# Output stage of a two-layer hybrid decoder: loads six items ahead, a written order on two engines, and weight sums spread over more ticks

## The chip, the cores and the metric

The kernel runs on one core of one Trainium2 chip. Its time is that of one execution on the device in microseconds; less is better. Five engines work side by side: TensorE (PE) multiplies matrices into PSUM, VectorE (DVE) and ScalarE (ACT) do elementwise work, GpSimd (POOL) does more of it, and SyncE (SP) issues the transfers (DMA). Each engine takes its instructions in the order in which they stand in its own queue, and waits at an instruction until what it needs is there.

## The reference

For each of two layers, with D_MODEL = SEQ = 1024 and D_INNER = 2048:

```python
h = rmsnorm(x, norm_g[l]) * (1.0 + scale[:, None, :]) + shift[:, None, :]
p = h @ w_in[l]
...                       # y_m: four mLSTM heads of 256, y_r: four retention heads of 256
y = jnp.concatenate([y_m, y_r], axis=-1) @ w_out[l]
x = x + gate[:, None, :] * y
```

At the end stands `rmsnorm(x, final_g)`. What the change touches is above all the product with `w_out[l]` (2048 x 1024), the sum into `x`, and the preparation of `w_out`.

## The kernel before, in words

*Precision.* Every factor is split into a high and a low half: ScalarE casts the high half (line 599), another engine subtracts it from the value (line 600). `mm3` then issues three matmuls, high x high, high x low and low x high (lines 134, 135, 136), 128 x 128 against 128 x 512.

*Heads.* A layer works through eight head groups: 0 to 3 are mLSTM, 4 to 7 retention. Each projects its columns of `w_in`, whose tiles come in through the tag `raw` (four buffers) and are split into `wH` and `wL` (six buffers each), and puts its y rows into DRAM (`ydr`). Loops advance a clock by ticks. Work that isn't urgent is a generator which `launch` puts in a list; it says at each `yield n` that it wants to go on n ticks later. A group of the later ones is some 32 ticks long.

*Weight sums.* The output product is computed by a scheme of seven products of half-size blocks in place of eight. It needs sums of blocks of `w_out`; `weight_sums` (line 899) forms these during the heads from tiles of the tag `g` (six buffers), which gates and y rows use too. Each of its 8 rounds has 5 steps with `yield 2`, so 80 ticks; it starts after group 3. Sums for products 5 and 6 go to `tdr`; for products 3, 7 and 4 both halves go to `tsp`.

*Output stage.* `out_projection` runs the products in the order 1, 2, 5, 6, 3, 7, 4. Each has eight items (one y tile and one weight tile each), and an item is 12 matmuls, three into each of four PSUM banks. Products 1 and 2 use the banks b1, products 5, 6 and 3 the banks b2, products 7 and 4 the banks b3. At a product's end its banks are copied (`save`, `sum_up`) or go into x rows (`out_rows`): multiply by the gate, add to the old x, store, square for the next norm. In `out_units` the last two items go bank by bank, so that a bank is finished, emptied and used by the next product while others are still at work.

`OutPrep` prepares the items. `stage` does all for one item at once: the load or sum of its y tile, the split of it, the loads of the weights and, where no halves are stored, their split. Three items are prepared before the first is taken, and `take` prepares one and hands out one. The weights of products 1, 2, 5 and 6 use `raw` (line 983) and split into `wH`/`wL`; stored halves are loaded into `wH`/`wL` straight away (line 979). y tiles come into the pool `b` of 62 tiles (line 943).

*Order.* TensorE's order is written out. The order of the other engines, SP's among them, is set by a planner that simulates the program on a timeline and puts each instruction at its estimated time; which buffers a tag has and which instruction waits for which release follow from it. `tc.manual_schedule(engines=...)` puts the named engines' instructions in the order of the program's text instead.

Of the kernel before, what the change touches and what calls it, by code (L numbers as in the profile page):

```python
# [69 lines left out]
def tile_hybrid_trunk(ctx, tc, x, c, positions, w_ada, b_ada, norm_g, w_in, conv_w, conv_b,  # L70
# [62 lines left out]
    def mm3(o, lt, rt, start, stop, more=False):  # L133
# [28 lines left out]
    tdr = [[[dpool.tile([P, HALF], F32, name=f"tdr{l}_{j}_{k}") for k in range(KT)] for j in range(8)]  # L162
           for l in range(DEPTH)]
    SPLIT = (3, 7, 4)
    tsp = [{p: [[dpool.tile([P, HALF], F32, name=f"tsp{l}_{p}_{k}_{w}") for w in range(2)] for k in range(KT)]
            for p in SPLIT} for l in range(DEPTH)]
    sdr = [[dpool.tile([P, HALF], F32, name=f"sdr{l}_{k}") for k in range(14)] for l in range(DEPTH)]
# [430 lines left out]
    def split_to(dst, src, eng=G):  # L598
        A.copy(dst[0], src)  # L599
        eng.tensor_tensor(dst[1], src, f(dst[0]), ALU.subtract)  # L600
# [295 lines left out]
                Q.dma_start(sdr[l][k], other)  # L896
            yield 2

    def weight_sums(l):
# [12 lines left out]
        for i in range(KT):  # L912
            w11, w12 = load(i, 0), load(i, 1)
            yield 2
            w22 = load(8 + i, 1)
            V.tensor_tensor(w11, w12, w11, ALU.subtract)
            Q.dma_start(tdr[l][5][i], w11)
            yield 2
            V.tensor_tensor(w12, w22, w12, ALU.subtract)
            V.tensor_tensor(w11, w22, w11, ALU.subtract)  # L920
            Q.dma_start(tdr[l][6][i], w11)
            keep(w22, 3, i)
            yield 2
            keep(w12, 7, i)
            w21 = load(8 + i, 0)
            yield 2
            V.tensor_tensor(w21, w21, w11, ALU.subtract)
            keep(w21, 4, i)
            yield 2

    class OutPrep:
        ORDER = (1, 2, 5, 6, 3, 7, 4)

        def __init__(self, l):
            self.l, self.ready = l, []
# [13 lines left out]
        def split(self, src, tiles):  # L949
            split_to(tiles, src, V)  # L950
            return tiles

        def stage(self, n=1):
            l, sub = self.l, ALU.subtract
            for p, i in self.todo[:n]:
                if p == 1:
                    src = self.y(i, 0)
                elif p == 2:
                    self.y12[i] = src = self.y(8 + i, 0)
                elif p == 5 and i < 6:  # L960
                    src = self.load(sdr[l][8 + i])
                elif p == 5:
                    src = self.load(ydr[l][i][1])
                    self.y22[i] = self.y(8 + i, 1)
                    V.tensor_tensor(src, src, self.y22[i], ALU.add)
                elif p == 6:
                    self.s2[i] = src = bt()
                    V.tensor_tensor(src, self.y22[i], self.s3[i], sub)
                elif p == 3:
                    src = self.y12[i]  # L970
                    V.tensor_tensor(src, src, self.s2[i], sub)
                else:
                    src = self.s3[i] if p == 7 else self.y22[i]
                y2 = self.split(src, (bt(F32R), bt(F32R)))
                last = p == 4 and i >= KT - 2
                w2 = (bt(F32R), bt(F32R)) if last else (wt("wH", 512, 6, F32R), wt("wL", 512, 6, F32R))
                if p in SPLIT:
                    for which in range(2):
                        Q.dma_start(f(w2[which]), tsp[l][p][i][which])
                else:  # L980
                    raw = wt("raw", 512, 4)
                    rows = slice((i if p == 1 else 8 + i) * P, (i + 1 if p == 1 else 9 + i) * P)
                    Q.dma_start(raw, w_out[l, rows, 0:512] if p < 3 else tdr[l][p][i])
                    self.split(raw, w2)
                self.ready.append((y2, w2))
                if self.early and (p > 1 or i > 3):
                    res, k, src = self.early.pop(0)
                    res[k] = self.load(src)
            del self.todo[:n]

        def take(self):
# [38 lines left out]
    def out_rows(l, half, cc, tt, bank, gb, xnew, ss, xr, copy=False):  # L1030
        row = half * 4 + tt
        tmp = wt("th", 512, 5)
        if copy:
            A.copy(tmp, bank)
        add_gated(xr, tmp if copy else bank, gb[cc], tmp)
# [15 lines left out]
    def out_projection(l, prep, gb, fg, nhT):  # L1051
# [10 lines left out]
        x12, x22, x21 = [None] * 4, [None] * 4, [None] * 4  # L1062
        b1 = [ps_p() for _ in range(4)]
        run_units(out_units(prep, b1, True, False, save(b1, c1, None)))
        x11 = [residual(l, 0, 0, tt) for tt in range(4)]
        run_units(out_units(prep, b1, False, True,
                            lambda tt: out_rows(l, 0, 0, tt, b1[tt], gb, xn[0], ss[0], x11[tt])))
# [3 lines left out]
        def sum_up(tt):  # L1071
# [128 lines left out]
    for l in range(DEPTH):  # L1200
# [85 lines left out]
        for hg in range(8):  # L1286
# [23 lines left out]
            if hg == 7:  # L1310
                run_units(gate_path(l, hg, hT, gp, 0, 1))
                loads = OutPrep(l)
                loads.stage(2)
                run_units(gate_path(l, hg, hT, gp, 1))
                loads.stage(1)
# [46 lines left out]
```

## Time and profile before

| | us |
|---|---|
| three runs, median | 2334.56 (2332.99 to 2337.56) |
| profiled execution, its own time | 2333.26 |
| its span in the trace | 2331.6 |
| TensorE busy | 2268.6 (97%) |
| VectorE busy | 1459.2 (63%) |
| ScalarE busy | 959.7 (41%) |
| GpSimd busy | 815.0 (35%) |

In the span, layer 0's output stage lies from about 1016 to 1191 us, layer 1's from about 2125 to the last matmul at 2321 us; the heads lie ahead of each. In rows of instructions, `L1059` is the line, `pp<-wH,b` what is written and read, `x2` how many were put together, and the brackets at the end give the idle time ahead of it and what ended that.

### The profile page before, as it was taken

The numbers are of one execution on the slowest core, as the hardware profiler recorded it, in microseconds if no ns is written. First come the engines' busy times: TensorE is split into PE (matmuls) and PEld (weight loads), VectorE is DVE, ScalarE is ACT, GpSimd is POOL, SyncE is SP. The second block draws the span as 40 slices with busy tenths as digits, with TensorE's granted clock in tenths as the row PEclk, the third lists the DMA queues.
The fourth block names the chain that finished last, engine by engine and source line by source line (L and its number), as shares of the span: only waits on it lengthen the run. The fifth ranks groups of instructions, "written<-read, shape, count | busy, mean of one in ns | idle before, by whom it ended". The sixth has DMA issues, their size and how long they took to land.

```text
span 2331.6 us, 35126 instructions
## 1 busy us (share of the span) xinstructions
PE 2268.6 (97%) x12405; PEld 1946.5 (83%) x12405; DVE 1459.2 (63%) x2971; ACT 959.7 (41%) x1868; POOL 815.0 (35%) x777
## 2 busy tenths in 40 slices
PE   5999999999999999999999999999999999999998
PEld 4878888889878989887878888888898888889876
DVE  7386678566685655557755765564656665555685
ACT  5535434444432333345344544444444333324452
POOL 0344344334353444310063434334433443442000
PEclk9999999999999999999999999999999999999999
DMA  7234434454675763566733334333447666535765
GB/s 246 70 79 118 120 91 144 112 180 129 210 247 188 248 194 99 168 197 197 251 108 77 75 106 123 104 113 104 135 136 243 198 210 216 151 104 179 244 208 180
DMA packets 385729, 367.52 MB, mean 158 GB/s; under 512 B 82421, under 2 KB 268541, under 8 KB 385553
## 3 DMA queue, kind: packets, MB, share of 16 engines
q1 hardware_dynamic: 385552, 365.28, 52.0%
q8 instruction: 97, 1.59, 0.3%
q14 instruction: 80, 0.65, 0.1%
HBM read 253.99 MB, written 111.18 MB: 157 GB/s over the span
## 4 chain that ended last, share of the span: by engine, by line
PE 66%; DVE 9%; DMA 9%; issue 6%; POOL 4%; ACT 3%; SPq 2%; POOLq 0%; DVEq 0%; ACTq 0%
PE pp L134 17%; PE pp L135 17%; PE pp L136 17%; PE pa L134 4%; PE pa L136 4%; PE pa L135 4%; DMA g<-in_w_out_dram 2%; POOL b L600 1%; DVE acc L617 1%; POOL wL L600 1%; DMA g<-gdr 1%; PE pa L751 1%; DMA b<-ydr 1%; DMA ndr<-zt 1%; DMA b<-in_w_ada_dram 1%
## 5 line engine op out<-in xcount | busy, mean ns | idle before, releaser
L134 PE MATMUL pp<-b,wH 128*128 128x512 f32 x1792 | 713.5, 398 | 1.1 <-ACT b L1232 1.1
L135 PE MATMUL pp<-b,wH 128*128 128x512 f32 x1792 | 709.1, 396 | 0.6 <-DVE b L1235 0.6
L136 PE MATMUL pp<-b,wL 128*128 128x512 f32 x1792 | 709.5, 396 | 0.0
L600 POOL TENSOR_TENSOR wL<-raw,wH 128x512 fp32r<-128x512 f32 x274 | 374.0, 1373 | 405.5 <-ACT wH L599 338.6
L136 PEld LDWEIGHTS pp<-b,wL 128*128 128x128 f32 x1792 | 338.7, 189 | 80.7
L134 PEld LDWEIGHTS pp<-b,wH 128*128 128x128 f32 x1792 | 339.2, 189 | 73.3 <-issue 1.5
L135 PEld LDWEIGHTS pp<-b,wH 128*128 128x128 f32 x1792 | 339.1, 189 | 72.9 <-DVE b L1235 1.4
L134 PE MATMUL pp<-wH,b 128*128 128x256 f32 (+1 forms) x1136 | 348.5, 307 | 5.6 <-ACT acc L1059 4.3
L136 PE MATMUL pp<-wH,b 128*128 128x256 f32 (+1 forms) x1136 | 347.3, 306 | 0.0
L135 PE MATMUL pp<-wL,b 128*128 128x256 f32 (+1 forms) x1136 | 346.5, 305 | 0.0
L600 POOL TENSOR_TENSOR b<-acc,b 128x256 fp32r<-128x256 f32 (+1 forms) x208 | 212.6, 1039 | 281.4 <-ACT b L599 277.6
L599 ACT CAST wH<-raw 128x512 fp32r<-128x512 f32 x338 | 207.5, 617 | 177.6 <-PE pp L135 113.1
L134 PEld LDWEIGHTS pp<-wH,b 128*128 128x128 f32 x1136 | 214.6, 189 | 17.6 <-ACT acc L1059 5.6
L136 PEld LDWEIGHTS pp<-wH,b 128*128 128x128 f32 x1136 | 214.2, 189 | 10.8
L135 PEld LDWEIGHTS pp<-wL,b 128*128 128x128 f32 x1136 | 214.4, 189 | 10.4
L617 DVE SCALAR_TENSOR_TENSOR acc<-pp,cols,acc 128x511 f32<-128x511 f32 (+2 forms) x192 | 142.3, 741 | 25.0 <-ACT acc L612 22.8
L599 ACT CAST b<-acc 128x256 fp32r<-128x256 f32 (+1 forms) x208 | 94.5, 486 | 131.3 <-DVE acc L694 82.3
L600 POOL TENSOR_TENSOR sL<-th,sH 128x384 fp32r<-128x384 f32 x64 | 67.9, 1061 | 127.2 <-ACT sH L599 118.8
L600 DVE TENSOR_TENSOR b<-b,b 128x512 fp32r<-128x512 f32 x112 | 78.2, 714 | 47.5 <-ACT b L599 47.1
L1104 POOL TENSOR_TENSOR rs<-s,mhalf 128x4 f32<-128x4 f32 (+1 forms) x9 | 7.8, 872 | 270.9 <-DVE s L1103 270.9
L134 PE MATMUL pa<-b,b 128*128 128x256 f32 (+1 forms) x320 | 91.7, 286 | 7.8 <-ACT nd L797 7.4
L600 POOL TENSOR_TENSOR cL<-cf,cH 128x516 fp32r<-128x516 f32 (+1 forms) x48 | 64.8, 1350 | 90.5 <-ACT cH L599 90.5
(287 smaller groups left out, 3796.8 us busy)
## 6 DMA issues: line engine op xcount, KB each, us to landing
raw<-in_w_in_dram SPq DMA_DIRECT2D x274, 256.0 KB
b<-in_w_ada_dram SPq DMA_DIRECT2D x96, 256.0 KB
tsp<-g SPq DMA_DIRECT2D x96, 256.0 KB
gdr<-g SPq DMA_DIRECT2D x64, 256.0 KB
ndr<-zt SPq DMA_DIRECT2D x128, 128.0 KB
g<-ndr SPq DMA_DIRECT2D x64, 256.0 KB
g<-gdr SPq DMA_DIRECT2D x64, 256.0 KB
g<-in_w_out_dram SPq DMA_DIRECT2D x64, 256.0 KB
```

The source lines that it names most:

```text
L134: PE.matmul(o, lt[0], rt[0], start=start, stop=False, skip_group_check=more)
L135: PE.matmul(o, lt[0], rt[1], start=False, stop=False, skip_group_check=more)
L136: PE.matmul(o, lt[1], rt[0], start=False, stop=stop, skip_group_check=more)
L599: A.copy(dst[0], src)
L600: eng.tensor_tensor(dst[1], src, f(dst[0]), ALU.subtract)
L617: V.scalar_tensor_tensor(acc[:, d:], pt[:, 0:HALF - d], wcol, acc[:, d:], ALU.mult, ALU.add)
L751: PE.matmul(pd, kk[i][:, jo + P:jo + CH], qd, start=dt == 0 and i == 0, stop=dt == 1 and i == 1)
L1104: G.tensor_tensor(rs[:, 0:n], s, mhalf[:, 0:n], ALU.pow)
```

## The change

1. `OutPrep.stage` becomes four steps, `fetch`, `sum_up`, `cast` and `low`, each with a queue behind it (`got`, `summed`, `halved`, `ready`). `fetch` issues the loads of up to three more items than before. Weights and stored halves are loaded into the pool `b`, no longer into `raw`, `wH` or `wL`; only the splits of products 1, 2, 5 and 6 use `wH`/`wL`.
2. After product 1 the steps move one item on (`sum_up` twice, `cast` once), so that from then on the sum, the cast and the low half of one item belong to different calls of `take`.
3. From there to the first row of product 4's end, VectorE and ScalarE follow the order of the text.
4. Product 7's banks are all copied by ScalarE at once; the rows they go into are worked through later, one per tick (`corner_later`).
5. `weight_sums` takes its pace as an argument: 3 ticks a step from after group 3 in layer 0 (120 ticks), 5 ticks a step from after group 1 in layer 1 (200 ticks).

The number of instructions of each engine and the bytes moved are the same in both.

```diff
-            yield 2
+            yield pace
...
-                    raw = wt("raw", 512, 4)
                     rows = slice((i if p == 1 else 8 + i) * P, (i + 1 if p == 1 else 9 + i) * P)
-                    Q.dma_start(raw, w_out[l, rows, 0:512] if p < 3 else tdr[l][p][i])
-                    self.split(raw, w2)
-                self.ready.append((y2, w2))
+                    w2 = self.load(w_out[l, rows, 0:512] if p < 3 else tdr[l][p][i])
+                self.got.append((p, i, src, w2))
...
+        def cast(self):
+            if not self.summed:
+                return
+            p, src, w2 = self.summed.pop(0)
+            halves = [(src, (bt(F32R), bt(F32R)))]
+            if p not in SPLIT:
+                halves.append((w2, (wt("wH", 512, 6, F32R), wt("wL", 512, 6, F32R))))
+                w2 = halves[1][1]
+            for x, t in halves:
+                A.copy(t[0], x)
+            self.halved.append((halves, (halves[0][1], w2)))
+
+        def low(self):
+            if not self.halved:
+                return
+            halves, ready = self.halved.pop(0)
+            for x, t in halves:
+                V.tensor_tensor(t[1], x, f(t[0]), ALU.subtract)
+            self.ready.append(ready)
...
         def take(self):
-            self.stage()
+            self.fetch(2 if len(self.got) < AHEAD else 1)
+            for step in (self.sum_up, self.cast, self.low):
+                step()
             return self.ready.pop(0)
...
         run_units(out_units(prep, b1, True, False, save(b1, c1, None)))
+        for step in (prep.sum_up, prep.sum_up, prep.cast):
+            step()
+        ordered = tc.manual_schedule(engines={mybir.EngineType.DVE, mybir.EngineType.Activation})
+        ordered.__enter__()
...
-        run_units(out_units(prep, b3, True, False,
-                            lambda tt: out_rows(l, 1, 1, tt, b3[tt], gb, xn[1], ss[1], x22[tt], True)))
+        corner = [None] * 4
+
+        def read_out(tt):
+            corner[tt] = wt("th", 512, 5)
+            A.copy(corner[tt], b3[tt])
+
+        def corner_later():
+            for tt in range(4):
+                out_rows(l, 1, 1, tt, corner[tt], gb, xn[1], ss[1], x22[tt], corner[tt])
+                yield 1
+
+        run_units(out_units(prep, b3, True, False, read_out))
+        launch(corner_later())
 
         def end(tt):
+            if tt == 0:
+                ordered.__exit__(None, None, None)
...
-            if hg == 3:
-                launch(weight_sums(l))
+            if hg == (1 if l else 3):
+                launch(weight_sums(l, 5 if l else 3))
```

How this moves instructions is seen at three places. Lines from the diff on are renumbered: 943 is 944 after, 979 is 966, 685 to 695 are 686 to 696, 916 to 920 are 917 to 921.

SP's queue in product 1 of layer 0, before (`ydr` are y tiles, `sdr` sums of them, `in_w_out_dram` output weights):

```order
L943 DMA b_2191_11695<-ydr0_10_0_245 128x512
L983 DMA raw_2233_11852<-in_w_out_dram 128x512
L943 DMA b_2197_11707<-sdr0_6_511 128x512
L943 DMA b_2214_11787<-ydr0_11_0_247 128x512
L983 DMA raw_2242_11883<-in_w_out_dram 128x512
L943 DMA b_2220_11799<-sdr0_7_512 128x512
L943 DMA b_2221_11813<-ydr0_12_0_249 128x512
```

and after:

```order
L944 DMA b_2178_11645<-ydr0_10_0_245 128x512
L852 DMA ndr0_7_0_109<-zt_2098_11335 32x8x128 x4
L944 DMA b_2179_11647<-in_w_out_dram 128x512
L533 DMA gdr0_7_1_1_158<-g_2109_11402 128x512
L944 DMA b_2180_11649<-sdr0_6_511 128x512
L944 DMA b_2185_11671<-ydr0_11_0_247 128x512
L944 DMA b_2186_11673<-in_w_out_dram 128x512
L944 DMA b_2187_11675<-sdr0_7_512 128x512
L944 DMA b_2193_11699<-ydr0_12_0_249 128x512
```

The weights go to `b` tiles, so that no load of this row of items asks for a `raw` buffer, and the y tiles 10 and 11 are now asked for around stores of group 7 (`ndr`, `gdr`), which before stood elsewhere.

VectorE's queue in group 4 of layer 0, before:

```order
L685 TENSOR_TENSOR acc_7608<-pp_7576,dm_7228 128x512
L686 TENSOR_TENSOR acc_7609<-pp_7576,kw_7234 128x512
L916 TENSOR_TENSOR g_7704<-g_7706,g_7704 128x512
L919 TENSOR_TENSOR g_7706<-g_7802,g_7706 128x512
L920 TENSOR_TENSOR g_7704<-g_7802,g_7704 128x512
L692 TENSOR_TENSOR th_7658<-pp_7627,nd_7231 128x512
L693 TENSOR_TENSOR th_7659<-pp_7627,dm_7225 128x512
```

and after:

```order
L686 TENSOR_TENSOR acc_7579<-pp_7554,dm_7220 128x512
L687 TENSOR_TENSOR acc_7580<-pp_7554,kw_7226 128x512
L693 TENSOR_TENSOR th_7629<-pp_7604,nd_7223 128x512
L694 TENSOR_TENSOR th_7630<-pp_7604,dm_7217 128x512
L695 TENSOR_TENSOR acc_7547<-acc_7547,th_7629 128x512
```

The three weight sums (916, 919, 920) no longer stand between the two halves of the rotary work on the k rows.

SP's queue towards the end of product 4 in layer 0, before:

```order
L401 DMA raw_2604_13380<-in_w_in_dram 128x256
L401 DMA raw_2607_13388<-in_w_in_dram 128x256
L401 DMA raw_2610_13396<-in_w_in_dram 128x256
L979 DMA b_2532_13034<-tsp0_4_6_0_453 128x512
L979 DMA b_2533_13035<-tsp0_4_6_1_454 128x512
L401 DMA raw_2613_13404<-in_w_in_dram 128x256
L979 DMA b_2540_13065<-tsp0_4_7_0_455 128x512
```

and after:

```order
L966 DMA b_2496_12870<-tsp0_4_6_0_453 128x512
L966 DMA b_2497_12871<-tsp0_4_6_1_454 128x512
L966 DMA b_2500_12878<-tsp0_4_7_0_455 128x512
L966 DMA b_2501_12879<-tsp0_4_7_1_456 128x512
L1056 DMA b_2506_12902<-in_x_dram 128x512
L1068 DMA xdr4_91<-b_2411_12511 128x512
```

The last stored halves of product 4 no longer stand behind the next layer's first weights (line 401).

More of the change, by code (lines that the diff above doesn't have):

```diff
@@ L897, in gated_later, with weight_sums @@
             yield 2
-    def weight_sums(l):
+    def weight_sums(l, pace):
         def load(k, cc):
@@ L917, in weight_sums @@
             Q.dma_start(tdr[l][5][i], w11)
-            yield 2
+            yield pace
             V.tensor_tensor(w12, w22, w12, ALU.subtract)
@@ L934, in __init__ @@
         def __init__(self, l):
-            self.l, self.ready = l, []
+            self.l, self.got, self.summed, self.halved, self.ready = l, [], [], [], []
             self.todo = [(p, i) for p in self.ORDER for i in range(KT)]
@@ L947, in y, with fetch @@
             return self.load(ydr[self.l][k][half]) if k < 14 else gated(self.l, 7, k - 14, half, bt())
[L949 to L954, printed above, removed]
+        def fetch(self, n=1):
+            l = self.l
             for p, i in self.todo[:n]:
+                src = None
                 if p == 1:
@@ L964, in stage @@
                     self.y22[i] = self.y(8 + i, 1)
[L965 to L976, printed above, removed]
                 if p in SPLIT:
+                    w2 = tuple(bt(F32R) for _ in range(2))
                     for which in range(2):
@@ L989, in stage, with split, sum_up @@
             del self.todo[:n]
+        def split(self, src, tiles):
+            split_to(tiles, src, V)
+            return tiles
+        def sum_up(self):
+            if not self.got:
+                return
+            p, i, src, w2 = self.got.pop(0)
+            if p == 5 and i > 5:
+                V.tensor_tensor(src, src, self.y22[i], ALU.add)
+            elif p == 6:
+                self.s2[i] = src = bt()
+                V.tensor_tensor(src, self.y22[i], self.s3[i], ALU.subtract)
+            elif p == 3:
+                src = self.y12[i]
+                V.tensor_tensor(src, src, self.s2[i], ALU.subtract)
+            elif p in (7, 4):
+                src = self.s3[i] if p == 7 else self.y22[i]
+            self.summed.append((p, src, w2))
@@ L991, in take, with begin @@
+        def begin(self, n):
+            self.fetch(n)
+            for step in (self.sum_up, self.cast, self.low):
+                for _ in range(n):
+                    step()
         def take(self):
-            self.stage()
+            self.fetch(2 if len(self.got) < AHEAD else 1)
+            for step in (self.sum_up, self.cast, self.low):
+                step()
             return self.ready.pop(0)
@@ L1028, in add_gated, with out_rows @@
         V.tensor_tensor(xr, xr, tmp, ALU.add)
-    def out_rows(l, half, cc, tt, bank, gb, xnew, ss, xr, copy=False):
+    def out_rows(l, half, cc, tt, bank, gb, xnew, ss, xr, tmp=None):
         row = half * 4 + tt
[L1032 to L1035, printed above, removed]
+        tmp = wt("th", 512, 5) if tmp is None else tmp
+        add_gated(xr, bank, gb[cc], tmp)
         if l < DEPTH - 1:
```

17 lines of the change are left out of this document (10 added, 7 removed).

## The prediction

> **What bounds the kernel now.** I read the busy time of the engines by stage first: layer 0's heads, its output stage, layer 1's heads, its output stage, the tail. The columns are length, then busy time and count of TensorE (PE), weight loads, VectorE, ScalarE and GpSimd, then granted clock, DMA share and GB/s.
>
> ```profile
> 120.00:1016.00 896.00, 884.94 (x5000) 768.12 (x4999) 588.32 (x1253) 352.27 (x692) 364.62 (x339) 0.99 0.52 155
> 1016.00:1191.00 175.00, 168.55 (x759) 135.85 (x758) 119.86 (x194) 76.23 (x145) 25.97 (x18) 0.98 0.67 214
> 1191.00:2125.00 934.00, 927.75 (x5249) 805.32 (x5248) 544.76 (x1134) 380.35 (x743) 384.18 (x368) 1.00 0.48 139
> 2125.00:2321.40 196.40, 193.90 (x904) 158.87 (x902) 132.86 (x238) 82.87 (x161) 13.40 (x14) 1.00 0.62 205
> 2321.40:2331.60 10.20, 0.00 (x0) 0.00 (x0) 4.91 (x11) 2.86 (x5) 1.08 (x2) 0.62 0.41 154
> ```
>
> TensorE is busy nearly throughout, so it is the bound, and no matmul is added or removed. Only its gaps can be won: 175.00 - 168.55 = 6.45 us and 196.40 - 193.90 = 2.50 us in the two output stages, 896.00 - 884.94 = 11.06 and 934.00 - 927.75 = 6.25 us in the heads. The 10.20 us tail runs the same code in both kernels, so I leave it.
>
> Next, what PE waited for (total, times, longest), in layer 0's output stage:
>
> ```profile
> PE pp L134 <- ACT acc L1059: 3.8, 2, 2.6
> PE pp L134 <- DMA b<-tsp: 1.3, 1, 1.3
> PE pa L134 <- ACT b L599: 0.6, 1, 0.6
> PE pp L135 <- DMA b<-tsp: 0.6, 1, 0.6
> ```
>
> and in layer 1's:
>
> ```profile
> PE pp L134 <- DVE g L529: 1.3, 1, 1.3
> PE pa L134 <- ACT b L599: 0.6, 1, 0.6
> PE pp L134 <- ACT acc L1059: 0.5, 1, 0.5
> ```
>
> Layer 0's 6.3 us are five waits, and 3.8 of them are for the copies (line 1059) that empty product 1's banks for product 2. PE's records there, in order of start:
>
> ```profile
> 1048.83 0.50 PE L134 MATMUL pp<-wH,b 128*128 128x512 f32 x1 [1.17 <-ACT acc L1059]
> 1052.39 0.80 PE L134 MATMUL pp<-wH,b 128*128 128x512 f32 x1 [2.60 <-ACT acc L1059]
> 1052.99 0.63 PE L135 MATMUL pp<-wL,b 128*128 128x512 f32 x1
> ...
> 1057.25 0.49 PE L136 MATMUL pp<-wH,b 128*128 128x512 f32 x1
> 1057.58 0.40 PE L134 MATMUL pp<-wH,b 128*128 128x512 f32 x1
> 1057.82 0.39 PE L135 MATMUL pp<-wL,b 128*128 128x512 f32 x1
> ```
>
> The stall has an aftermath. From 1052.39 to 1057.58 twelve matmuls start, in 5.19 us; at the normal distance, which the last two rows show (0.24 us by their rounded times, 0.232 on average over a product), they take 2.78. The slow dozen costs 5.19 - 2.78 = 2.4 us beyond the idle time. Why were the copies late? ScalarE:
>
> ```profile
> 1043.72 1.07 ACT L1059 COPY acc<-pp 128x512 f32<-128x512 f32 x2
> 1047.68 0.62 ACT L599 CAST b<-b 128x512 fp32r<-128x512 f32 x1 [2.89 <-DMA b<-ydr]
> 1048.20 0.58 ACT L1059 COPY acc<-pp 128x512 f32<-128x512 f32 x1
> 1051.76 0.58 ACT L1059 COPY acc<-pp 128x512 f32<-128x512 f32 x1
> ```
>
> Between the copies stands a cast of a y tile that has not landed; ScalarE waits 2.89 us for that DMA with the third copy behind it. The load was late because SP, which issues every load in order, stood still:
>
> ```profile
> 1029.51 0.32 SPq L943 DMA_DIRECT2D b<-ydr  x1
> 1038.63 0.33 SPq L983 DMA_DIRECT2D raw<-in_w_out_dram  x1
> ```
>
> SP's own waits over the whole stage:
>
> ```profile
> SPq L983 <- DVE wL L600: 32.4, 18, 6.8
> SPq L979 <- PE pa L136: 17.6, 12, 2.8
> SPq L401 <- POOL wL L600: 7.4, 3, 3.2
> ```
>
> For 9.1 us nothing was issued: the weight load of line 983 wants one of four `raw` buffers, and the next y loads queue behind it. Over layer 0's output stage SP waited 32.4 us in this way, 17.6 us for TensorE to release `wH`/`wL`, and 7.4 us with the next layer's loads (line 401), which stand ahead of the last stored-half loads; those are the `b<-tsp` waits of 1.3 and 0.6 us. The data path is therefore the cause: items are prepared three ahead, 3 x 12 x 0.232 = 8.4 us, and a 9.1 us block uses that up.
>
> **The change part by part.** *Loads.* The changed program has the same number of instructions on every engine and the same bytes. Output weights and stored halves now go to the large `b` pool and are asked for up to three items earlier, so the lead is about 16.7 us; waits of line 983 on `raw` cannot occur, nor those of line 979 on `wH`/`wL`. The last tsp loads stand ahead of the next layer's loads.
>
> *Written order.* Per item the steady work beside twelve matmuls (2.78 us) goes by these group rows of layer 0's output stage:
>
> ```profile
> L599 ACT CAST b<-b 128x512 fp32r<-128x512 f32 x50 | 29.7, 619 | 21.9 <-DMA b<-ydr 12.8 <-DVE b L968 7.5 <-DVE b L965 0.8
> L600 DVE TENSOR_TENSOR b<-b,b 128x512 fp32r<-128x512 f32 x50 | 36.9, 749 | 19.3 <-ACT b L599 19.3
> ```
>
> ScalarE makes at most two casts, 2 x 0.62 = 1.24 us. VectorE makes at most a sum and two low halves, about 3 x 0.75 = 2.25 us. Both fit under TensorE, with only 0.5 us left on VectorE where residual rows are added as well; three ready items cover a lag of 8.4 us there. In the written order sum, cast and low half of one item stand in different steps, so the 19.3 us that VectorE idled for casts should largely go.
>
> *At product 1's end* four copies are still placed by the planner. In the changed order three stand together and the fourth follows two casts whose data were asked for six items earlier: at worst 1.2 us late, hidden by the order of PE's first item (bank 3 comes last, 9 matmuls = 2.1 us after bank 0).
>
> Sum for the output stages: idle 6.45 + 2.50, aftermath 2.4, together 11.35. I leave the 1.3 us wait for `g` of line 529 (it lies before the written stretch), hence **-10**. Bounds: -11.4 if all goes, 0 if each wait reappears elsewhere.
>
> *Weight sums, layer 0.* They now run at 3 ticks a step rather than 2. In group 4 before:
>
> ```profile
> 670.29 0.69 DVE L916 TENSOR_TENSOR g<-g,g 128x512 f32<-128x512 f32 x1
> 673.17 0.69 DVE L920 TENSOR_TENSOR g<-g,g 128x512 f32<-128x512 f32 x1 [1.47 <-DMA tdr<-g]
> 673.78 0.68 DVE L692 TENSOR_TENSOR th<-pp,nd 128x512 f32<-128x512 f32 x1
> ```
>
> and on PE:
>
> ```profile
> 677.73 0.39 PE L136 MATMUL pa<-b,b 128*128 128x256 f32 x1 [0.86 <-POOL b L600]
> 680.64 0.39 PE L136 MATMUL pa<-b,b 128*128 128x256 f32 x1 [2.29 <-POOL b L600]
> 682.48 0.63 PE L135 MATMUL pp<-b,wH 128*128 128x512 f32 x1
> ```
>
> Three weight sums, one of them waiting 1.47 us until a store has read its tile, stand before line 692, whose result goes through ScalarE and GpSimd to PE: VectorE turns to it 673.78 - 670.29 = 3.5 us late, and PE loses 0.86 + 2.29, then about eight matmuls at 0.43 instead of 0.23 us (records of 0.63 us, as above): 3.15 + 8 x 0.195 = 4.7 us. In the changed order nothing of the sums stands there (two of that round stand among the same group's q rows, far behind the store that they must wait for); about 0.5 us may stay, since GpSimd still has a `wL` between the two halves. I take **-4.5**, bounds 0 and -5.
>
> *Weight sums, layer 1*, start two groups earlier and take 5 ticks a step, 200 ticks in all instead of 80. Their clashes now show as waits for `cL`, layer 0 and layer 1:
>
> ```profile
> PE pa L135 <- POOL cL L600: 1.0, 1, 1.0
> PE pa L135 <- POOL cL L600: 2.8, 3, 1.0
> ```
>
> One on VectorE in layer 1:
>
> ```profile
> 1751.76 0.69 DVE L916 TENSOR_TENSOR g<-g,g 128x512 f32<-128x512 f32 x1 [1.32 <-DMA g<-in_w_out_dram]
> ```
>
> A sum waits 1.32 us for its weights ahead of the state update (line 778) that `cL` is made from. Removing that is worth between 0 and 3.8 us; I take **-1**, as the planner places them anew and one such wait is all I can tie to a row. Against it stands what the trace does not show: the sums now run beside the mLSTM groups 2 and 3 and hold tiles of the six `g` buffers longer, which the z and o gates and the y stores also use. Nearest rows: the 1.3 us wait for `g` above, and the whole stall of 4.7 us. I put it at **+1**, near the short wait, bounds 0 and +5.
>
> Sum: -10 - 4.5 - 1 + 1 = -14.5. The profiled run took 2333.26 us (its span 2331.6), 1.3 below the median of the runs, 2334.56. From the median: 2334.56 - 14.5 = **2320 us**.
>
> [...]
>
> **Rivals.** *B, only the output stage gains.* The planner orders the heads anew, and stalls like group 4's arise elsewhere; the 11.06 and 6.25 us of gaps in the heads show how common they are; against it, group 4's order is clean. 2334.56 - 10 = 2324.6.
>
> *C, the largest stall stays.* Product 1's copies are outside the written order; if a cast or normalisation still delays one past the bank's turn, 1.17 + 2.60 + 2.4 = 6.2 us remain: 2326. For it: the copies stood between casts before too. Against: what they waited for was a late load.
>
> *D, slower.* The layer-1 sums in groups 2 and 3 hold `g` tiles, an evacuation on VectorE or ScalarE waits for a `g` buffer, and PE idles over 2.2 us each time, at 4.7 us with the aftermath. Three such stalls eat the gain, and from five on the kernel is clearly slower: 2320 + 5 x 4.7 = 2343.5. For it: some six groups instead of three, six buffers, longer holds. Against: VectorE was busy only 58% of layer 1's heads (544.76 of 934), and a slower pace leaves more room between sums.
>
> *E, waits move.* More loads outstanding at 214 GB/s and 0.67 DMA share, and a strict order in which one late tile blocks a whole engine: new waits equal the old ones, 2331 to 2335. For it: VectorE's margin of 0.5 us per item. Against: same bytes, twice the lead.
>
> [...]
>
> **How the numbers follow.** Forecast 0.50, B 0.17, C 0.10, E 0.11, F 0.04, D 0.08. A measurement of this kernel can tell about 0.2% (4.7 us) from no change. Faster than 2329.9: the forecast, B, C, F, and a little of E, 0.82; the same, most of E, 0.10; slower, D, 0.08. The lower end adds what is left of the output idle (1.3) and of the `cL` waits (2.8), drops the +1, and allows about 4 us for head gaps that the new order may close: 2320 - 9 = 2311. The upper end reaches past C into E: 2331.
>
> **What would show it.** Right: no PE wait on copies of product 1 over 1.5 us, output-stage idle below about 2 us, no row of 0.63 us behind 1052 or 682, SP without waits on `raw` in the output stage, group 4 without a weight sum before the chain of line 692 (693 in the new numbering). Wrong: a new PE wait of over 2 us followed by slow matmuls in layer 1's groups 2 and 3, VectorE waiting for `g` there, or waits on casts or low halves inside products 2 to 4.

## The result, and the profile after

The changed kernel takes 2317.98 us (median of four runs, 2315.29 to 2319.17) against 2333.77 us beside it; the ratio is 0.9931, interval 0.9912 to 0.995. On a second chip it took 2317.12 us against 2327.95, 0.9953 (0.9938 to 0.9968): 15.8 us less on the one, 10.8 us on the other. The forecast was 2320 us, and faster.

Busy time by stage in the changed kernel, the columns as in the prediction; the stages are layer 0's heads, its output stage, layer 1's heads, its output stage:

```profile
120.00:1016.00 896.00, 886.21 (x5016) 770.40 (x5014) 590.65 (x1258) 352.85 (x696) 362.98 (x339) 1.00 0.53 158
1016.00:1181.00 165.00, 163.69 (x747) 134.55 (x748) 125.21 (x191) 75.53 (x142) 25.34 (x18) 0.99 0.63 215
1181.00:2113.00 932.00, 927.25 (x5263) 806.88 (x5262) 550.62 (x1136) 375.47 (x741) 381.51 (x366) 1.00 0.47 139
2113.00:2306.90 193.90, 191.22 (x889) 157.00 (x887) 135.25 (x237) 84.87 (x164) 16.75 (x16) 1.00 0.63 213
```

TensorE's idle time in these stretches is now 165.00 - 163.69 = 1.31 and 193.90 - 191.22 = 2.68 us (6.45 and 2.50 before). All that PE waited for in layer 0's output stage, and in layer 1's:

```profile
PE pp L134 <- DVE g L530: 1.8, 1, 1.8
```

```profile
PE pp L134 <- DVE g L530: 1.7, 1, 1.7
PE pp L136 <- POOL wL L601: 0.6, 1, 0.6
PE pp L134 <- ACT wH L600: 0.2, 1, 0.2
```

The waits for product 1's copies, for casts of items and for stored halves are gone. What is left is the last z gate (line 530) at the entry, which in layer 0 is new; the 0.6 and 0.2 us in layer 1 are for input weights of the last head group, ahead of the stage.

Group 4 of layer 0, where PE had lost 0.86 and 2.29 us, on PE:

```profile
676.59 0.28 PE L134 MATMUL pa<-b,b 128*128 128x256 f32 x1
676.71 0.28 PE L135 MATMUL pa<-b,b 128*128 128x256 f32 x1
676.83 0.28 PE L136 MATMUL pa<-b,b 128*128 128x256 f32 x1
```

The three matmuls follow one another at 0.12 us.

TensorE runs the same number of matmuls in almost the same order in all these kernels, so that times between the starts of the same two matmuls, counted from the first, say where time went. In us, from PE's records; "again" is the changed kernel on the second chip, the last three columns are experiments told of below:

```
matmuls        stretch                         before   after   again | paces  output  early
0-500          start                           116.89  118.23  119.82  119.79  117.78  118.79
500-3400       layer 0, up to group 4's stall  528.01  527.38  528.02  529.85  527.40  527.92
3400-3600      group 4's stall                  47.58   41.78   41.78   41.78   47.34   41.78
3600-5510      rest of layer 0's heads         322.91  327.03  327.53  326.34  324.80  324.93
5510-5665      entry, end of product 1          28.72   30.39   28.84   28.73   28.76   28.76
5665-6250      products 2 to 4                 142.72  131.88  131.89  135.94  131.87  131.91
6250-9000      layer 1, first part             508.34  508.26  505.88  505.54  507.04  506.22
9000-11500     layer 1, the later groups       426.47  422.25  421.77  423.05  426.97  420.75
11500-11677    entry of its output stage        31.50   32.89   32.82   31.60   32.44   31.97
11677-12404    its output stage                164.90  163.46  163.59  165.99  165.53  161.39
```

Against before, products 2 to 4 of layer 0 took 10.8 us less, group 4 5.8 less, layer 1's later groups 4.2 less and its output stage 1.4 less. Given back were 4.1 us in the rest of layer 0's heads, 1.7 at the end of product 1 (in this execution) and 1.4 at layer 1's entry.

The entry in layer 0, on SP, ScalarE, VectorE and PE in turn:

```profile
997.00 0.38 SPq L327 DMA_DIRECT2D raw<-in_w_in_dram  x1
997.47 0.46 SPq L944 DMA_DIRECT2D b<-ydr  x1
```

```profile
1005.15 0.62 ACT L1005 CAST b<-b 128x512 fp32r<-128x512 f32 x1 [2.64 <-DMA b<-ydr]
```

```profile
1016.57 0.68 DVE L530 SCALAR_TENSOR_TENSOR g<-th,pp 128x512 f32<-128x512 f32 x1
```

```profile
1017.30 0.74 PE L134 MATMUL pp<-wH,b 128*128 128x512 f32 x1 [1.84 <-DVE g L530]
1017.84 0.63 PE L135 MATMUL pp<-wL,b 128*128 128x512 f32 x1
```

SP had issued nothing since 991.0, until a `raw` buffer for the last input weights came free; y tiles stand behind. ScalarE then waits 2.64 us for one, with the gate's work queued behind it, and PE waits 1.84 us and runs slow matmuls (records of 0.63 us). It looks like the chain of the first kernel's stall, at another place; but 9 us of work of ScalarE and VectorE lie between the late cast and the gate, so these rows alone do not show it. The last experiment tests it.

### The profile page after: what moved, and what is told of

Its sections match the earlier page's. It is cut to its first block, busy times and chain, and to the rows that moved or that the text cites. A ratio compares the mean times of both kernels' runs of the same rounds, so it can differ in the third digit from the quotient of the medians.

```text
span 2317.5 us, 35197 instructions
## 1 busy us (share of the span) xinstructions
PE 2262.3 (98%) x12405; PEld 1948.0 (84%) x12405; DVE 1473.7 (64%) x2971; ACT 955.8 (41%) x1868; POOL 813.3 (35%) x777
## 5 line engine op out<-in xcount | busy, mean ns | idle before, releaser
L134 PE MATMUL pp<-wH,b 128*128 128x256 f32 (+1 forms) x1024 | 302.8, 296 | 3.6 <-DVE g L530 3.6
L136 PE MATMUL pp<-wH,b 128*128 128x256 f32 (+1 forms) x1024 | 302.6, 295 | 0.0
L135 PE MATMUL pp<-wL,b 128*128 128x256 f32 (+1 forms) x1024 | 302.1, 295 | 0.0
L600 ACT CAST wH<-raw 128x512 fp32r<-128x512 f32 x274 | 167.2, 616 | 155.3 <-PE pp L135 116.2
L134 PEld LDWEIGHTS pp<-wH,b 128*128 128x128 f32 x1024 | 193.2, 189 | 10.2 <-DVE g L530 4.4
L135 PEld LDWEIGHTS pp<-wL,b 128*128 128x128 f32 x1024 | 193.3, 189 | 5.5
L136 PEld LDWEIGHTS pp<-wH,b 128*128 128x128 f32 x1024 | 193.0, 188 | 5.7
L134 PE MATMUL pa<-b,b 128*128 128x256 f32 (+2 forms) x384 | 117.3, 305 | 10.1 <-ACT nd L798 8.1
L136 PE MATMUL pa<-b,b 128*128 128x256 f32 (+2 forms) x384 | 116.5, 303 | 0.0
L135 PE MATMUL pa<-b,b 128*128 128x256 f32 (+2 forms) x384 | 116.3, 303 | 0.0
```

What stands on the lines that cost most here:

```text
L134: PE.matmul(o, lt[0], rt[0], start=start, stop=False, skip_group_check=more)
L135: PE.matmul(o, lt[0], rt[1], start=False, stop=False, skip_group_check=more)
L136: PE.matmul(o, lt[1], rt[0], start=False, stop=stop, skip_group_check=more)
```

## The experiments

**The paces alone.**

```diff
-    def weight_sums(l):
+    def weight_sums(l, pace):
...
-            if hg == 3:
-                launch(weight_sums(l))
+            if hg == (1 if l else 3):
+                launch(weight_sums(l, 5 if l else 3))
```

> The kernel before with the new paces of the weight sums alone (3 ticks in layer 0, 5 ticks from after group 1 in layer 1). My theory: the two parts of the change gain separately; in the trace of the changed kernel group 4 of layer 0 is 5.5 us shorter and layer 1's heads some 4 us, of which some 3 us may be lost again at the entry of layer 0's output stage, where y loads set the time: 2333.8 - 9.5 + 3 = about 2327, with the 2.60 us wait for product 1's copies still there. Rival 'all of it is the output stage': 2333 to 2335. Rival 'the heads gain and nothing is lost later': 2324.

Measured: 2320.84 us beside 2329.79, ratio 0.9958 (0.9946 to 0.997). The table's column "paces" has group 4 at 41.78 and layer 1's later groups 3.4 us shorter. But products 2 to 4 of layer 0 are 6.8 us shorter too, without any edit to them: the stall at product 1's copies did not occur. SP and ScalarE there:

```profile
1031.46 0.38 SPq L943 DMA_DIRECT2D b<-ydr  x1
1038.44 0.33 SPq L983 DMA_DIRECT2D raw<-in_w_out_dram  x1
```

```profile
1043.22 0.62 ACT L599 CAST b<-b 128x512 fp32r<-128x512 f32 x1 [2.08 <-DMA b<-ydr]
1043.75 1.07 ACT L1059 COPY acc<-pp 128x512 f32<-128x512 f32 x2
1045.51 0.62 ACT L599 CAST b<-b 128x512 fp32r<-128x512 f32 x1 [0.69 <-DMA b<-ydr]
1047.17 0.59 ACT L1059 COPY acc<-pp 128x512 f32<-128x512 f32 x1 [1.04 <-PE pp L136]
```

SP still stands still for 7.0 us and ScalarE still waits for y tiles; but the second one lands 2.2 us sooner (cast at 1045.51, not 1047.68), and the third copy waits for PE itself. The stall of 1048 was thus a near miss of a late transfer, and not a wall. I had expected 6.5 us less than before (2327 of 2333.8), with that stall in place; it was 9.0, without it.

**The output part alone.**

```diff
-            if hg == (1 if l else 3):
-                launch(weight_sums(l, 5 if l else 3))
+            if hg == 3:
+                launch(weight_sums(l, 2))
```

> The changed kernel with the old paces (2 ticks, after group 3, in both layers). My theory: the waits inside layer 0's output stage go (11 us by the two traces), the stall in group 4 stays (0.86 + 2.29 us and slow matmuls), and the entry to the output stage has no wait because PE comes later: 2333.8 - 11 = about 2323. Rival 'all of it is the output stage': 2318. Rival 'the parts need each other': 2328 or more.

Measured: 2322.78 us, ratio 0.9966 (0.9953 to 0.9979): 7.0 us less than before beside it, where I had expected 10.8. Products 2 to 4 take 131.87 us, as in the changed kernel; group 4's stall stays (47.34), and layer 1's later groups are as before (426.97). What is lost lies at the entry, where I had expected no wait:

```profile
PE pp L134 <- DVE g L530: 1.8, 1, 1.8
```

So it comes with the output part and not from PE being early. In the profiled executions the parts gain 9.5 and 8.2 us to the last matmul, the whole 14.5: less than the sum, since each alone removes the stall at product 1's copies.

**Without the written order.**

```diff
-        ordered = tc.manual_schedule(engines={mybir.EngineType.DVE, mybir.EngineType.Activation})
-        ordered.__enter__()
...
-            if tt == 0:
-                ordered.__exit__(None, None, None)
```

> The changed kernel without the written order on VectorE and ScalarE: the planner orders them in the output stage too; loads, steps and paces as changed. My theory: late loads were the cause of the stalls, so the order matters little: 2317 to 2321, and no PE wait over 1 us inside the output stages. Rival 'the written order is what keeps casts off the copies': the wait for product 1's copies or waits on casts come back, 2324 to 2328.

Measured: 2316.71 us, ratio 0.9938 (0.9916 to 0.9961): the same as the change. Products 2 to 4 take 131.78 us. The planner's order is as good here.

**Loads three ahead.**

```diff
-    AHEAD = 3
+    AHEAD = 0
```

> The changed kernel with loads three items ahead, as before, but into the pool b (sum, cast and low half of an item fall into one call again, in written order). My theory: SP's stop at a raw buffer was what used up the lead, so without it three items (8.4 us) nearly do: 2318 to 2322. Rival 'the longer lead does it': waits on casts and loads come back inside the products of layer 0 and layer 1, 2325 to 2332. Rival 'sum, cast and low half in one call starve PE in written order': over 2335.

Measured: 2346.18 us, ratio 1.0062 (1.0042 to 1.0081), slower than before. The third expectation came true. With nothing fetched beyond, the steps after product 1 have nothing to move, and sum, cast and low half fall into one call. PE and ScalarE in products 5 to 3 (the second fence: ScalarE's waits in total, times, longest):

```profile
1130.54 0.79 PE L134 MATMUL pa<-b,b 128*128 128x512 f32 x1 [4.29 <-ACT g L1108]
```

```profile
ACT b L1005 <- DVE b L991: 18.2, 8, 5.1
ACT b L1005 <- DVE b L988: 12.8, 7, 2.8
```

In the written order ScalarE's cast waits for VectorE's sum, up to 5.1 us when residual rows stand before it, with the bank copies (line 1108) behind. The two residual rows ahead of that sum:

```profile
1123.29 1.78 DVE L1060 TENSOR_TENSOR th<-acc,b 128x512 f32<-128x512 f32 x1
1125.10 1.67 DVE L1061 TENSOR_TENSOR b<-b,th 128x512 f32<-128x512 f32 x1
```

They take 1.78 and 1.67 us, where these lines mostly take 0.69: GpSimd works on four splits (line 601) from 1119.76 to 1126.22, and the two rows run beside them (the last section counts such rows). That is 2.1 of the 5.1 us. Two causes were mixed in this run; the next two part them.

**Six ahead, but one call.**

```diff
-        for step in (prep.sum_up, prep.sum_up, prep.cast):
-            step()
```

> The changed kernel without the three steps after product 1: loads stay up to six items ahead and the order written, but sum, cast and low half of an item fall into one call again. It tells apart what the run with three items ahead mixed. Theory 'the written order needs the steps apart' (there ScalarE's casts waited for VectorE's sums, up to 5.08 us): the stage from product 2 on takes 140 us or more in layer 0 (131.9 in the changed kernel), the whole 2328 to 2346. Rival 'it was the lead': 2316 to 2320, and under 134 us from product 2 on.

Measured: 2333.24 us, ratio 1.0024 (1.0013 to 1.0035): the first theory. Products 2 to 4 take 142.1 us with the same waits (`ACT b L1005 <- DVE b L991` 15.1 us in 6 times). The three steps are worth 142.1 - 131.9 = 10 us where the order is written; the longer lead, 148.4 - 142.1 = 6 us under that order.

**Three ahead, the planner's order.** The two edits above on the written order and on `AHEAD` together.

> The changed kernel with loads three ahead and the planner's order in place of the written one; loads into the pool b and paces as changed. Theory 'with SP free of raw buffers three items suffice': layer 0 from product 2 on within 2 us of the changed kernel's 131.9 us, but the entry 2 to 4 us longer, since y loads are asked for later: 2318 to 2322. Rival 'the lead is what removes the waits': 137 us or more from product 2 on, 2325 or more.

Measured: 2317.98 us, ratio 0.9955 (0.9939 to 0.997), beside 2317.12 us and 0.9953 for the changed kernel on that chip. Products 2 to 4 take 131.91 us. Only the entry is worse: PE waits 3.4 us for the last z gate in place of 2.4. So neither the longer lead nor the written order carries the gain; together, and with the steps apart, they do no harm, and the written order without the steps does.

**Only the output weights into the pool `b`**, on the kernel before:

```diff
-                    raw = wt("raw", 512, 4)
+                    raw = bt()
```

> The kernel before with one edit: the output weights of products 1, 2, 5 and 6 are loaded into the pool b in place of the four raw buffers. Loads three ahead, the planner's order and the old paces stay. My theory: SP's 9.1 us stop at a raw buffer is what delays the y loads, so the 1.17 + 2.60 us waits for product 1's copies and the slow matmuls behind go: 6 us less than before, 2325 to 2329, the tsp waits at the stage's end stay. Rival 'three items ahead is too little in any case': within 2 us of before.

Measured: 2346.23 us, ratio 1.0069 (1.0054 to 1.0084). My theory of the total fell, that of the place held: between product 1 and product 2 PE waits no more. Products 2 to 4 take 142.0 us all the same, with waits for a cast (1.8 us) and low halves (1.2 us) in product 5 and for a stored half at the end (1.6 us). The larger loss is at the heads' end, on PE and on SP:

```profile
1009.82 0.79 PE L134 MATMUL pp<-b,wH 128*128 128x512 f32 x1 [4.36 <-ACT wH L599]
```

```profile
997.07 0.32 SPq L943 DMA_DIRECT2D b<-ydr  x1
997.60 0.32 SPq L532 DMA_DIRECT2D gdr<-g  x1
998.01 0.38 SPq L983 DMA_DIRECT2D b<-in_w_out_dram  x1
1001.41 0.32 SPq L943 DMA_DIRECT2D b<-ydr  x1
1005.37 0.33 SPq L983 DMA_DIRECT2D b<-in_w_out_dram  x1
```

SP's waits around there (978 to 1036 us):

```profile
SPq L943 <- PE pa L751: 11.3, 2, 11.1
SPq L983 <- PE pa L136: 3.7, 1, 3.7
```

Before, four weight loads were out by 987.2 in `raw` buffers, which are free by then, and the first y load at 991.8. With the weights in `b` nothing goes out until TensorE releases a tile: SP stands 11.1 us at the first y load (line 943), with the weights behind it, and 3.7 us at a weight load. ScalarE waits for these transfers ahead of the last input weights' cast. The same happens in layer 1 (4.30 us).

**The stored halves into `b` as well.**

```diff
-                last = p == 4 and i >= KT - 2
-                w2 = (bt(F32R), bt(F32R)) if last else (wt("wH", 512, 6, F32R), wt("wL", 512, 6, F32R))
+                w2 = (bt(F32R), bt(F32R)) if p in SPLIT else (wt("wH", 512, 6, F32R), wt("wL", 512, 6, F32R))
```

> As the run that loads the output weights into b, and the stored halves of products 3, 7 and 4 go into b too. My theory: the waits for stored halves at the end of layer 0's output stage (0.57 + 1.27 us) go as well: 8 to 9 us less than before, 2322 to 2327, that is, buffers alone give most of what the output part of the change gives. Rival 'lead and steps are needed': 2329 or more.

Measured: 2342.89 us, ratio 1.0053 (1.0038 to 1.0068). The waits for stored halves are gone, as expected; the loss at the heads' end stays, and products 2 to 4 take 137.13 us, with waits in product 5. PE's waits from 980 to 1200 us:

```profile
PE pp L134 <- ACT wH L599: 4.4, 1, 4.4
PE pa L134 <- ACT wH L599: 1.8, 1, 1.8
PE pa L134 <- ACT zt L1058: 1.3, 1, 1.3
PE pa L135 <- DVE wL L600: 0.9, 1, 0.9
PE pp L134 <- DVE g L529: 0.6, 1, 0.6
```

Buffers alone, then, do not make the change. What parts this kernel from the one with three loads ahead in the planner's order is the code of an item (both loads take their `b` tiles ahead of the halves, and two items are fetched before either is split), product 7's rows put off, and the paces. Which of these brings the first loads forward was not tried alone. For products 2 to 4 the paces aren't needed: the output part alone has the old ones and takes 131.87 us.

**Gate rows one group earlier.** VectorE's 4.13 us wait for `w_ada` stands before PE's 1.69 us wait in group 6 of the changed kernel.

```diff
-            if hg == 5:
+            if hg == (5 if l else 4):
                 launch(gate_rows(l, gb))
```

> The changed kernel with layer 0's gate rows (sums over w_ada, whose late loads VectorE waits 4.13 us for just before PE's 1.69 us wait in group 6) started one group earlier. My theory: the head groups lose to transfers what group 4 gained, so that 1.69 us goes but the wait at the output stage's entry grows by about as much: within 1.5 us of the change, 2316 to 2319.5. Rival 'the waits are independent': 1.5 to 2 us less. Rival 'two streams of sums now clash in group 5': 2320 or more.

Measured: 2315.82 us, ratio 0.9939 (0.9924 to 0.9954). The total cannot tell it from the change. By place: the rest of layer 0's heads takes 324.67 us, 2.4 less than in the changed kernel, and the entry wait did not grow but fell to 1.1 us, so the rival "independent" has layer 0. Layer 1, which the edit does not name, lost 2.7 us between matmuls 11000 and 11500, with the same kind of wait that had left layer 0:

```profile
PE pa L134 <- ACT n L840: 1.7, 1, 1.7
```

The order was not at fault: in the traces VectorE, ScalarE, GpSimd and SP work through layer 1 in the changed kernel's order (buffer numbers left out). What did not move is a transfer. VectorE waits there for a `w_ada` load until 2030.06 us, 6.94 us long; in the changed kernel until 2030.24, 4.66 us long. PE starts the matmul behind at 2039.14 and 2039.37. What PE had gained by then, it spent waiting for a load that came when it had come before.

**Five items' loads early.** On the changed kernel:

```diff
             if hg == 7:
+                loads = OutPrep(l)
+                loads.fetch(5)
                 run_units(gate_path(l, hg, hT, gp, 0, 1))
-                loads = OutPrep(l)
-                loads.begin(2)
+                for step in (loads.sum_up, loads.cast, loads.low):
+                    step()
+                    step()
                 run_units(gate_path(l, hg, hT, gp, 1))
-                loads.begin(1)
+                for step in (loads.sum_up, loads.cast, loads.low):
+                    step()
```

> The changed kernel with the loads of the first five output items issued before group 7's z gate, ahead of two input-weight loads at which SP stands still. In the changed kernel PE waits 1.84 us for the last z gate at the entry of layer 0's output stage and twelve slow matmuls follow (4 us in all), because ScalarE waits 2.64 us for a y tile ahead of that gate's work. My theory: these 4 us go and layer 1's entry (1.72 us) shortens: 2313 to 2316. Rival 'the time is only put off': a wait of the same length comes up inside product 1 or 2, 2317 to 2319. Rival 'earlier output loads delay the head's own': slower than the change by 2 us or more.

Measured: 2312.22 us beside 2331.26, ratio 0.9925 (0.9908 to 0.9941), under the range that I gave. It was run again beside the changed kernel:

> The changed kernel as it is, beside the version that loads five output items early on one chip: 0.6 to 0.8% under the kernel before, as measured.

> The version that issues the loads of five output items before group 7's z gate, again, on one chip with the changed kernel. Theory: 4 to 6 us under the changed kernel (1.84 us idle and 12 slow matmuls at layer 0's entry, 1.72 us at layer 1's), its interval apart from that of the change. Rival 'the earlier difference was the chip': within 2 us of it.

Measured: 2309.43 us for it, ratio 0.9918 (0.9903 to 0.9933); 2317.12 us and 0.9953 (0.9938 to 0.9968) for the changed kernel. The intervals lie apart; it beats both kernels, the change by 7.7 us, more than the 4 to 6 expected. Its two output stages:

```profile
1016.00:1180.00 164.00, 164.00 (x756) 134.39 (x755) 126.14 (x190) 75.09 (x142) 25.25 (x18) 1.00 0.62 212
...
2105.00:2297.60 192.60, 192.33 (x897) 158.23 (x896) 135.31 (x240) 85.02 (x165) 16.16 (x16) 1.00 0.63 215
```

TensorE is busy in 164.00 of 164.00 and 192.33 of 192.60 us: the entry waits of both layers are gone, as they would be if the late y loads had caused them. In the table, against the changed kernel on that chip: 2.6 us in the rest of layer 0's heads, 1.0 in layer 1's later groups, 0.9 at its entry and 2.2 in its output stage, that is 6.7 of a difference of 7.5 us to the last matmul.

## Why the prediction was right, and where its steps were off

The direction and the main terms were right. That the total came within 2 us, 2320 against 2318, is luck: errors cancelled, and on the second chip the gain was 10.8 us where 14.5 was forecast. The kernel before took 2322.95 to 2337.56 us in all its executions, the changed one 2315.04 to 2323.38, and each column of the table is one execution. Step by step:

*Output stages, -10.* Products 2 to 4 gained 10.8 us and layer 1's output stage 1.4; the wait for line 529's `g` stayed, as assumed. The mechanism, a late y load behind SP's wait for a `raw` buffer (9.1 us without an issue, then 2.89 us of ScalarE's wait for the tile), is what the trace of the kernel before shows. The prediction follows it to the third copy; the longer wait, 2.60 us, was for the fourth. VectorE and ScalarE in the kernel before:

```profile
1048.33 0.69 DVE L600 TENSOR_TENSOR b<-b,b 128x512 fp32r<-128x512 f32 x1 [3.23 <-ACT b L599]
1050.84 1.02 ACT L839 ACTIVATE n<-pa,nmu,rsd 128x256 f32<-128x256 f32 x2 [1.54 <-DVE nmu L836]
```

VectorE waits 3.23 us for the cast of the late tile, with a norm behind it; ScalarE then waits 1.54 us for that norm, with the fourth copy behind. So the late tile held this copy too, by way of VectorE. That the `raw` wait alone made it late no run shows by itself: the stall is gone without that wait (the output weights in `b`), but there PE comes to the stage 14 us later, and it is gone with the paces alone, where SP still stands at `raw` for 7.0 us. A block of 7.0 us is shorter than the lead of 8.4 and one of 9.1 is longer, which fits the estimate, but two cases do not make a limit. And the doubled lead, which I counted as the cure, isn't needed: three ahead gives 131.91 us. What does it, of the item's new code and product 7's late rows, stays open. Of the written order I said that it fits, and that VectorE's 19.3 us of waits for casts should largely go. It fits with the steps apart; with sum, cast and low half in one call the kernel is 0.2% to 0.6% slower than before. The 19.3 us fell to 5.4, but that was worth nothing: with three ahead in the planner's order they are 21.3 us (1016 to 1181), and the stage is as short.

*At product 1's end*: no wait on copies, as forecast.

*Group 4, -4.5*: 5.8 us, beyond my bound of 5. The half microsecond that I left for GpSimd's `wL` did not stay.

*What was missing*: what PE gained in group 4 it met again. From there to the entry 4.1 us came back. In the changed kernel PE waits here:

```profile
912.78 0.39 PE L134 MATMUL pa<-b,b 128*128 128x256 f32 x1 [1.69 <-ACT n L840]
```

In the run with the old paces PE starts the same matmul at 915.84 and has not waited for it; with the paces alone it waits 1.7 us again. Behind it stands a `w_ada` load that came when it had come before: VectorE's wait for it ends at 903.69 us after a wait of 4.13, in the kernel before at 904.06 after 1.70. Starting the gate rows a group earlier takes PE's wait away. The other part is the entry, 1.84 us, which is there with the output part alone and not with the paces alone. My sum priced such new waits only for layer 1.

*Layer 1's sums, -1 + 1*: 4.2 us gained in the later groups, and nothing lost in groups 2 and 3. All that PE waited for from 1181 to 2113 us:

```profile
PE pa L134 <- ACT nd L798: 2.0, 1, 2.0
PE pa L494 <- DVE b L484: 1.2, 1, 1.2
PE pa L135 <- POOL cL L601: 1.0, 1, 1.0
PE pp L135 <- POOL b L601: 0.3, 1, 0.3
PE pa L134 <- ACT n L840: 0.2, 1, 0.2
```

The gain is beyond my bound of 3.8. The waits for `cL` went from 2.8 to 1.0 us, where I dared take one, and a wait of 0.7 us for a low half of GpSimd's went too; rival D, slower by `g` buffers, has no row.

So -10 - 4.5 - 1 + 1 = -14.5 became -12.2 - 5.8 - 4.2 + 4.1 + 1.7 + 1.4 = -15.0, and with +0.9 from the other stretches and the tail, -14.1 us of span (2331.6 to 2317.5). Rival B, "only the output stage gains", falls by the table: group 4 and layer 1's later groups gave 10.0 us, and 4.1 came back in layer 0's heads. The runs agree: on one chip the output part alone took 2322.78 us and the whole, in the planner's order, 2316.71. (That the paces alone gave 0.42% proves less, as 6.8 us of it lay in products 2 to 4.) C falls; E appears only in its mild form, in group 6 and at the entry.

*The signs that I named*: no row of 0.63 us behind the two old places, no weight sum before the chain of line 693, and no output load waits for `raw` (the next layer's loads still do, for 2.3 us in place of 7.4). PE's idle in the two stages is 1.84 and 1.72 us, each below 2, but not together.

*The slow matmuls* went with the idles, as the sums assumed with 2.4 us for the output stage and 8 x 0.195 us for group 4. F in the chances, a cause other than the idles, falls with that. In the changed kernel an idle of 1.84 us at layer 0's entry has slow ones behind it (1017.84, 0.63 us). The last section has more on it.

## What to carry to other kernels

An engine that takes its work in order passed on a late transfer to what stood behind it (ScalarE's 2.89 us wait for one y tile held a copy, and VectorE's 3.23 us wait for the cast held the next), so look at what stands ahead of the load on the issuing queue and behind the wait on the engine, and ask where the loads' buffers come free: the cheap repair (buffers from a bigger pool) lost 0.7% because no tile of that pool was free at the moment that counted (SP stood 11.1 us at the first y load), and issuing a few loads before the stage gained 0.3%. Here a written order did no harm only with producer and consumer of one item in different steps. And a gain on the bounding engine was paid in full only as far as the next wait that its lateness had hidden: both `w_ada` loads came at the same time as before (VectorE's waits ended at 903.69 us against 904.06, and at 2030.06 against 2030.24), and the earlier PE waited for them, 1.7 us each time. Compare starts of the same instruction, not sums, to see it.

## What the runs showed of the hardware

**The clock.** Whether TensorE came back slow was not settled by the length of its idle. In the profiled execution an idle of 1.84 us at layer 0's entry is followed by slow matmuls (0.63 us records, quoted above). In another execution of the same program:

```profile
1019.88 0.50 PE L134 MATMUL pp<-wH,b 128*128 128x512 f32 x1 [2.42 <-DVE g L530]
1020.23 0.40 PE L135 MATMUL pp<-wL,b 128*128 128x512 f32 x1
```

2.42 us, and no slow one behind it: that stretch took 28.84 us in place of 30.39.

The granted clock goes with it. In the profiles of the kernel before and of the changed kernel it changes, up to the last matmul, only between full and half, and from one change to the next it is always a whole multiple of 3.41 us: before, 365.23 us at full and 6.83 us at half are 107 and 2 of them; after, 665.60 and 3.41 us are 195 and 1. Two neighbouring steps of that length in the first execution, and two in the other (length, TensorE's busy time and matmuls, granted clock, DMA share, GB/s):

```profile
1013.98:1017.39 3.41, 1.57 (x8) 1.00 1.01 340
1017.39:1020.81 3.42, 3.42 (x13) 0.50 1.06 386
```

```profile
1015.84:1019.25 3.41, 1.63 (x8) 1.00 0.87 297
1019.25:1022.66 3.41, 2.78 (x17) 1.00 1.05 398
```

The idle of 1.84 us lies whole in one step, and the next step runs at half clock. Of the 2.42 us, 1.79 lie in one step and 0.63 in the next, and the clock stays. Take all such steps at full clock from 80 us to the last matmul. The profiles of the kernel before and of the changed kernel have 1295: the seven with the most idle, 1.84 to 2.67 us, are each followed by a step at half clock, and of the other 1288, with up to 1.52 us, none is. Over all fourteen profiles of this case it is less clean: all 36 with more than 1.9 us of idle are followed by one, of the 9038 with less than 1.74 us one is, and of the 13 between four are. So what parts nearly all of them here is how much idle falls into one step. The price was one step at half clock, 3.41 us (1017.39 to 1020.81), or two, 6.83 us: in the kernel before, 1050.62 to 1057.45 us, the slow dozen. PE starts again 3.32 us after the begin of the first of the two steps in the one execution and 4.04 us after it in the other, so the steps lay differently against the same program, and the shorter wait was the slow one.

**VectorE beside GpSimd.** In the kernel before, none of VectorE's 536 `TENSOR_TENSOR` instructions of 128x512 with no `TENSOR_TENSOR` of GpSimd, of whatever shape, beside it took over 0.70 us. All 39 that took over 1.2 us, up to 1.8, had one beside it; so did all 47 in the changed kernel. Not every one that had is slow: 158 of 224 in the kernel before took at most 0.70 us.
